# A hybrid encoder layer on one core: block-diagonal matmuls in the DeltaNet recurrence, and where the fifth weight buffer lies

## The chip, the cores and the metric

The kernel runs on one core of one Trainium2 chip. The metric is the device time of one execution in microseconds (us), lower is better; the median of three runs stands for the kernel. The engines are TensorE (PE in the profile, with PEld for its weight loads), VectorE (DVE), ScalarE (ACT), GpSimd (POOL) and SyncE (SP), whose queue issues most of the DMAs.

## The reference

One layer over 16 meta tokens and 512 positions of width 1024, in float32. It is a SwiGLU feed-forward (inner width 2816), a hybrid mixer, and a second feed-forward, each between two RMSNorms and added to the residual `h`:

```
h = h + 0.5 * rmsnorm(swiglu(rmsnorm(h, n[0]), ffn1_wi, ffn1_wo), n[1])
h = h + rmsnorm(hybrid_mixer(rmsnorm(h, n[2]), ...), n[3])
h = h + 0.5 * rmsnorm(swiglu(rmsnorm(h, n[4]), ffn2_wi, ffn2_wo), n[5])
```

The mixer projects its input once, runs a Fourier branch, a short-convolution branch and a gated DeltaNet branch, projects each to 1024, adds them under sigmoid gates and applies one output projection. The DeltaNet branch has 4 heads of 128, runs over chunks of 64 positions, forward and backward in time, and sums the directions. In a chunk, `t` is the inverse of a unit triangular 64x64 matrix, and `attn` is a 64x64 decay-masked attention:

```
def step(S, xs):
    attn_n, u_n, w_n, qd_n, kd_n, gl_n = xs
    v_new = u_n - w_n @ S
    o = qd_n @ S + attn_n @ v_new
    S = S * gl_n[..., None, None] + jnp.swapaxes(kd_n, -1, -2) @ v_new
    return S, o
```

with `u = t @ v_beta` and `w = t @ (k_beta * exp(gc))`.

## The kernel before, in words

**Layout and arithmetic.** Activations lie transposed: channels in 8 blocks of 128 partitions, positions along the free axis. A large matmul is done as three fp32r matmuls: each weight tile and each activation is split into a high part, rounded to fp32r, and a low remainder (`mm`, lines 251 to 257). `load` (line 229) brings a weight tile of 128 x 1024 by DMA into a staging tile `ws` (two buffers), then ACT casts it into `wh` (line 239) and DVE subtracts to get `wl` (line 240). `wh` and `wl` come from the pool `wp`, with five buffers each. All matmuls are issued on line 153, so the profile tells them apart by their tiles: `pb` and `pd` are the two sets of four PSUM banks.

**Order.** PE's instructions run in the order in which the program issues them. The order on the other engines is laid out ahead of time by the tile scheduler from its own cost model, from priorities (`load` is put 150 places ahead, evictions marked urgent further) and from when buffers come free; on the chip each engine then keeps that order and waits at its head. Side work of the mixer (the recurrence, the Fourier transform) is written as generators: `T.at` adds up a modelled PE time for every matmul, and `tick`, called between groups of projection matmuls, resumes a generator once `T.at` has passed the time at which it asked to go on. A `yield SC` asks for 1.8 us after the work issued so far.

**Stages.** The first feed-forward (`ffn`) computes most of its first product by a seven-product (Strassen) scheme over pairs of weight blocks: `pair_load` (line 596) loads two blocks, forms sums on DVE and takes three tile pairs from `wp` and one half-size pair `w4`. `edge` (line 403) crosses to the next stage: it finishes the last output tiles (`tail`), computes the norm, and starts the first products of the next stage with weights (`nxt`) loaded ahead. The mixer follows (`mixer`, line 866), whose units are one weight tile against all positions; then `edge` again, the second feed-forward, and `finish`. Every stage opens pools of its own (`gp` for a feed-forward, `mp` and `dp` for the mixer), which are closed at the edge. In the mixer the eight tiles of the output projection (`A["wout"]`) come last: five in a loop and three in `tail`, in both halves of the positions.

**The recurrence** (`dn_core`, line 1273) runs twice, for heads 0 and 1 and for heads 2 and 3. It builds the masked matrices `A_` and `at` (lines 1323 and 1324), inverts the triangular ones by substitution on DVE into `Z` (which shares the slot `EZ` with earlier tiles, and is named EZ in the profile), and takes eight steps `s`. A step handles four chains: heads `j` = 0, 1 and directions `d` = 0 (chunk `c = s`) and 1 (`c = 7 - s`). Two chunks share the 128 partitions: chunk `c` lies in half `hf = c % 2`, rows `X`, so the two directions of one head are always in opposite halves. A step has three parts with a `yield SC` after each:

- `kq` against the state `Sst` (128x128, four matmuls; the profile's Sst,kq), then `vt` on DVE (line 1450) and the first half of the output `O`;
- four 64x64 matmuls with `Z` (profile: vp,EZ or vn,EZ), then `v1` by four ACT activations that scale by `beta` (line 1465); `vt` and `v1` share the tag `vp`;
- the update of the state, four matmuls of 64 rows by 128 columns with the decayed keys `kd` (tag `sub`; not in the last step), then four 64x64 matmuls with `at`, and the evictions on DVE.

At step 0 the backward chains have no state yet and use `vn` directly.

## Time and profile before

| | |
|---|---|
| median of 3 runs | 1278.52 us (1276.74 to 1278.81) |
| the profiled execution's own time | 1280.05 us |
| its span in the profile | 1278.2 us |
| mean granted TensorE clock | 0.998 |
| DMA | 129.27 MB, mean 101 GB/s |

In the profile a row of a group or of the timeline has the line, the engine, the operation, output<-inputs by tile tags, partitions x elements, and a count. For a matmul the first shape (128\*128, 64\*64, 64\*128) is rows by columns of the array in use. The timeline begins each row with its start and its length in us and ends, where the engine was idle before, with the idle time and what ended it. PE's lengths overlap, since matmuls are pipelined, so costs on PE are read from start to start. An f32 matmul (not fp32r) shows as two records.

### The profile page before, as it was taken

Reading aid. Unit: us, or ns where it says so; the run is one execution under the profiler, and the core shown is the slowest. Engines: PE = TensorE matmul, PEld = TensorE weight load, DVE = VectorE, ACT = ScalarE, POOL = GpSimd, SP = SyncE. Lnnn points to the kernel's source line nnn. Section 1 sums busy time; section 2 is a strip of 40 time slices with the busy share of each in tenths; the row PEclk is TensorE's granted clock in tenths of the full one; section 3 lists DMA queues with packets and bytes.
Section 4 is the critical chain, followed back from the end, with each engine's and each line's share of the span. In section 5 each row is a group of like instructions: output and inputs, shape, how many; then the busy total and the mean of one; then the engine's idle time right before and its main releaser. Section 6 shows DMA issues by size and latency. Waiting matters only on the chain.

```text
span 1278.2 us, 23021 instructions
## 1 busy us (share of the span) xinstructions
PE 1260.2 (99%) x9111; PEld 1155.5 (90%) x9111; DVE 943.3 (74%) x1883; ACT 616.9 (48%) x1201; POOL 13.5 (1%) x28
## 2 busy tenths in 40 slices
PE   9999999999989999999999999999999999999998
PEld 9999999999989988778998777887988999999997
DVE  7978777766568779768799678554779887777654
ACT  7665444434386452344643534334566644444436
POOL 0000000000000000000000000000200000000000
PEclk9999999999999999999999999999999999999999
DMA  7243333321254222422221313235423433333213
GB/s 245 74 143 106 99 99 99 98 96 59 83 187 149 84 78 68 110 77 68 84 67 59 78 48 91 82 94 179 161 87 94 146 100 100 100 100 95 79 50 132
DMA packets 70207, 129.27 MB, mean 101 GB/s; under 512 B 15820, under 2 KB 24140, under 8 KB 70100
## 3 DMA queue, kind: packets, MB, share of 16 engines
q1 hardware_dynamic: 64244, 124.14, 31.1%
q10 hardware_dynamic: 5088, 1.57, 0.5%
q0 software_dynamic: 768, 2.10, 0.4%
q8 instruction: 71, 1.16, 0.4%
q14 instruction: 36, 0.29, 0.1%
HBM read 120.41 MB, written 7.37 MB: 100 GB/s over the span
## 4 chain that ended last, share of the span: by engine, by line
PE 82%; DVE 10%; DMA 2%; ACT 2%; issue 2%; SPq 1%; DVEq 0%; ACTq 0%
PE pb L153 52%; PE pd L153 29%; PE pd L157 1%; DVE wl L245 1%; DMA wf<-in_wi 1%; DVE wl L240 1%; DVE s L414 1%; DVE x L421 1%; DVE acc L312 1%; DVE h L416 1%; DMA ws<-in_wab 1%; ACT wh L239 0%; DVE h L568 0%; DMA h<-in_xT 0%; DMA ws<-in_wout 0%
## 5 line engine op out<-in xcount | busy, mean ns | idle before, releaser
L153 PE MATMUL pb<-x,wh 128*128 128x264 f32 (+3 forms) x1584 | 353.9, 327 | 4.3 <-DVE x L421 1.8
L153 PEld LDWEIGHTS pb<-x,wh 128*128 128x128 f32 x1584 | 247.0, 189 | 33.0 <-issue 4.2
L153 PE MATMUL pb<-x,wl 128*128 128x264 f32 (+3 forms) x792 | 220.4, 323 | 0.0
L153 PE MATMUL pb<-gh,h 128*128 128x264 f32 (+2 forms) x816 | 191.3, 320 | 3.1 <-ACT pb L355 3.1
L153 PE MATMUL pd<-x,wh 128*128 128x264 f32 (+2 forms) x1040 | 192.1, 284 | 0.0
L239 ACT CAST wh<-ws 128x1024 fp32r<-128x1024 f32 (+1 forms) x110 | 105.1, 956 | 170.7 <-PE pb L153 145.7
L244 ACT CAST wh<-wf 128x1024 fp32r<-128x1024 f32 x108 | 113.5, 1051 | 149.2 <-PE pd L153 119.7
L245 DVE TENSOR_TENSOR wl<-wf,wh 128x1024 fp32r<-128x1024 f32 x108 | 131.8, 1222 | 43.4 <-ACT wh L244 42.5
L153 PEld LDWEIGHTS pd<-x,wh 128*128 128x128 f32 x1040 | 160.0, 188 | 1.7
L240 DVE TENSOR_TENSOR wl<-ws,wh 128x1024 fp32r<-128x1024 f32 (+1 forms) x110 | 121.1, 1102 | 37.9 <-ACT wh L239 37.6
L153 PEld LDWEIGHTS pb<-x,wl 128*128 128x128 f32 x792 | 134.6, 188 | 12.4 <-DVE wl L384 0.2
L153 PEld LDWEIGHTS pb<-gh,h 128*128 128x128 f32 x816 | 132.0, 189 | 13.6 <-ACT pb L355 3.7
L153 PE MATMUL pd<-x,wl 128*128 128x264 f32 (+2 forms) x520 | 143.8, 284 | 0.0
L153 PE MATMUL pb<-gl,h 128*128 128x264 f32 (+2 forms) x456 | 123.7, 314 | 0.0
L153 PEld LDWEIGHTS pd<-x,wl 128*128 128x128 f32 x520 | 96.2, 188 | 0.4
L153 PEld LDWEIGHTS pb<-gl,h 128*128 128x128 f32 x456 | 78.3, 189 | 4.3
L153 PE MATMUL pd<-h,wh 128*128 128x264 f32 (+1 forms) x294 | 82.1, 282 | 0.0
L153 PE MATMUL pd<-l,wh 128*128 128x264 f32 (+1 forms) x288 | 81.5, 283 | 0.0
L153 PE MATMUL pd<-h,wl 128*128 128x264 f32 (+1 forms) x288 | 81.4, 283 | 0.0
L698 DVE TENSOR_TENSOR y<-y,pb 128x264 f32<-128x264 f32 (+1 forms) x128 | 48.6, 420 | 30.8 <-PE pb L153 30.8
L239 ACT CAST h<-ws 128x1024 fp32r<-128x1024 f32 (+1 forms) x40 | 38.5, 968 | 60.3 <-PE pb L153 50.5
L153 PE MATMUL pb<-y,wh 128*128 128x512 f32 x192 | 61.3, 400 | 0.0
(325 smaller groups left out, 2295.4 us busy)
## 6 DMA issues: line engine op xcount, KB each, us to landing
wf<-in_wi SPq DMA_DIRECT2D x144, 256.0 KB, 2.6
ws<-in_wo SPq DMA_DIRECT2D x64, 256.0 KB, 3.0
ws<-in_win SPq DMA_DIRECT2D x32, 512.0 KB, 3.6
ws<-in_wg SPq DMA_DIRECT2D x24, 512.0 KB, 3.5
ws<-in_wi SPq DMA_DIRECT2D x13, 512.0 KB, 3.8
ws<-in_wo SPq DMA_DIRECT2D x32, 192.0 KB, 2.4
ws<-in_wout SPq DMA_DIRECT2D x8, 512.0 KB, 3.6
h<-in_xT SPq DMA_DIRECT2D x10, 264.0 KB, 5.3
```

What stands on the lines that cost most here:

```text
L153: return self.e.matmul(out, lhsT, rhs, **kw)
L157: return self.e.transpose(*a)
L239: nc.scalar.copy(h[:, :n], st[:, :n])
L240: nc.vector.tensor_tensor(l[:, :n], st[:, :n], h[:, :n].bitcast(F32), op=ALU.subtract)
L244: self.nc.scalar.copy(h, src)
L245: self.nc.vector.tensor_tensor(l, src, h.bitcast(F32), op=ALU.subtract)
L312: V.tensor_tensor(acc, acc, sq, op=ALU.add)
L414: V.scalar_tensor_tensor(t, ya[0][i][:, k, :W], self.gains[:, gpost, k:k + 1], r[:, c], op0=ALU.mult, op1=ALU.mult)
L416: V.tensor_tensor(hT[:, k, c], hT[:, k, c], t, op=ALU.add)
L421: V.scalar_tensor_tensor(x[1][:, k, c], hT[:, k, c], g, x[0][:, k, c].bitcast(F32), op0=ALU.mult, op1=ALU.subtract)
L698: V.tensor_tensor(y, y, p, op=ALU.add)
```

## The change

It has three parts.

**Blocks on the diagonal.** For one head and step, the forward and the backward 64x64 matrices lie on the diagonal of one 128x128 tile whose other quarters are zero. `at` is laid out so from the start (`[P, 2, 8, P]`, by head and step, cleared on GpSimd, and written in halves). For `Z`, a tile `ZB` (two steps deep) is cleared once, and ACT copies the two blocks of a step into it (`blocks`). `vt` and `v1` then hold both directions of a head in one 128-row tile; where a chain has no state, `vt` is a copy of `vn`. Four 64x64 matmuls become two 128x128 ones, at `Z` and at `at`. `v1` is two activations, scaled by `bB`, which holds `beta` by head and step.

**The weight pool.** `wp` has four buffers in place of five. In a feed-forward, a new function `wtile` takes every fifth tile from the stage's own pool `gp` (tags `wh5` and `wl5`, one buffer) and the others from `wp`; the edge switches this off, and the mixer has the four.

**The tail of the mixer.** The last three output tiles go into three buffers of their own (`th`, `tl`) in the pool `mm` that holds the merged branches.

```
-        self.wp = e(tc.tile_pool(name="wp", bufs=5))
+        self.wp = e(tc.tile_pool(name="wp", bufs=4))
...
+    def wtile(self, tag):
+
+        n = self.turn[tag] = (self.turn.get(tag, 0) + 1) % 5
+        if self.five and n == 0:
+            return self.t(self.gp, tag + "5", [P, KD, P], F32R)
+        return self.t(self.wp, tag, [P, KD, P], F32R)
...
-            h, l = to or (self.t(self.wp, "wh", [P, KD, P], F32R), self.t(self.wp, "wl", [P, KD, P], F32R))
+            h, l = to or (self.wtile("wh"), self.wtile("wl"))
...
+        self.five = False
         tiles, tx, tc, more = tail()
...
+        self.turn, self.five = {}, True
         return ctx
...
-            ws = [(m, self.load(A["wout"][m])) for m in range(KD - NT, KD)]
+            ws = [(m, self.load(A["wout"][m], to=[self.t(self.mm2, i, [P, KD, P], F32R, NT) for i in ("th", "tl")]))
+                  for m in range(KD - NT, KD)]
...
-        at = self.t(dp, "at", B4)
+
+        at = self.t(dp, "at", [P, 2, 8, P])
+        ZB = self.t(dp, "ZB", [P, 2, 2, P])
+        nc.gpsimd.memset(at, 0.0)
+        nc.gpsimd.memset(ZB, 0.0)
...
-                V.tensor_tensor(at[:, 2 * j + d], E[:, 2 * j + d], b[:, :, 1], op=ALU.mult)
+                for hf in range(2):
+                    X = slice(hf * 64, hf * 64 + 64)
+                    V.tensor_tensor(at[X, j, hf::2, X] if d == 0 else at[X, j, 1 - hf::2, X], E[X, 2 * j + d][:, ::1 - 2 * d],
+                                    b[X, ::1 - 2 * d, 1], op=ALU.mult)
...
+        bB = self.t(dp, "bB", [P, 2, 8])
+        for j, d in chains:
+            for hf in range(2):
+                X = slice(hf * 64, hf * 64 + 64)
+                V.tensor_copy(bB[X, j, (hf if d == 0 else 1 - hf)::2], beta[X, 2 * j + d, 0:4][:, ::1 - 2 * d])
+
+        def blocks(s):
+            for d in range(2):
+                c = s if d == 0 else 7 - s
+                X = slice((c % 2) * 64, (c % 2) * 64 + 64)
+                ACT.copy(ZB[X, s % 2, :, X], Z[X, d::2, c // 2])
+        blocks(0)
...
-            vt = self.t(dp, "vp", [P, 4, P], F32, 2)
+            vt = self.t(dp, "vp", [P, 2, P], F32, 2)
...
+                else:
+                    V.tensor_copy(vt[X, j], vn[X, j, t])
...
-            for j, d, hd, c, t, hf, X, Y, has in info:
-                T.matmul(b[X, hd * P:(hd + 1) * P], Z[X, hd, t], vt[X, hd] if has else vn[X, j, t], start=True, stop=True)
-            v1 = self.t(dp, "vp", [P, 4, P], F32, 2)
-            for j, d, hd, c, t, hf, X, Y, has in info:
-                ACT.activation(v1[X, hd], b[X, hd * P:(hd + 1) * P], AF.Copy, scale=beta[X, hd, t:t + 1])
+            for j in range(2):
+                T.matmul(b[:, j * P:(j + 1) * P], ZB[:, s % 2, j], vt[:, j], start=True, stop=True)
+            v1 = self.t(dp, "vp", [P, 2, P], F32, 2)
+            for j in range(2):
+                ACT.activation(v1[:, j], b[:, j * P:(j + 1) * P], AF.Copy, scale=bB[:, j, s:s + 1])
+            if s < 7:
+                blocks(s + 1)
...
-            for j, d, hd, c, t, hf, X, Y, has in info:
-                T.matmul(b[X, hd * P:(hd + 1) * P], at[X, hd, t], v1[X, hd], start=True, stop=True)
+            for j in range(2):
+                T.matmul(b[:, j * P:(j + 1) * P], at[:, j, s], v1[:, j], start=True, stop=True)
```

More of the change, by code (lines that the diff above doesn't have):

```diff
@@ L164, in __init__ @@
         self.sides = []
+        self.turn, self.five = {}, False
         self.T = Tensor(tc.nc)
@@ L371, in start @@
                self.t(self.wp, "wl", [P, KD, P], F32R)) for i in range(len(srcs))]
+        self.turn = {n: len(srcs) for n in ('wh', 'wl')}
         pieces = [slice(0, 1), slice(1, 2), slice(2, 4), slice(4, 6), slice(6, 8)]
@@ L607, in pair_load, with put @@
             nc.sync.dma_start(fc[:, hi], w2[:, hi])
-            def put(f, a, b, w=KD, tag="w", pool=self.wp, bufs=None):
-                h = self.t(pool, tag + "h", [P, w, P], F32R, bufs)
-                l = self.t(pool, tag + "l", [P, w, P], F32R, bufs)
+            def put(f, a, b, w=KD, new=self.wtile):
+                h, l = new(f"w{'4' if w < KD else ''}h"), new(f"w{'4' if w < KD else ''}l")
                 self.split(h, l, f[:, :w])
@@ L622, in pair_load @@
             V.tensor_tensor(fd[:, lo], fb[:, hi], fb[:, lo], op=ALU.add)
-            put(fd, 4, None, 4, "w4", self.gp, 2)
+            put(fd, 4, None, 4, lambda n: self.t(self.gp, n, [P, 4, P], F32R, 2))
         return out
@@ L952, in ready @@
             mm = self.dctx.enter_context(self.tc.tile_pool(name="mm", bufs=1))
+            self.mm2 = mm
             return self.t(mm, "mh", [P, KD, S], F32R), self.t(mm, "ml", [P, KD, S], F32R)
@@ L1449, in dn_core @@
                 if has:
-                    V.scalar_tensor_tensor(vt[X, hd], b[X, hd * P:(hd + 1) * P], neg_eg[X, hd, t:t + 1], vn[X, j, t],
+                    V.scalar_tensor_tensor(vt[X, j], b[X, hd * P:(hd + 1) * P], neg_eg[X, hd, t:t + 1], vn[X, j, t],
                                            op0=ALU.mult, op1=ALU.add)
+                else:
+                    V.tensor_copy(vt[X, j], vn[X, j, t])
             for j, d, hd, c, t, hf, X, Y, has in info:
@@ L1470, in dn_core @@
                 for j, d, hd, c, t, hf, X, Y, has in info:
-                    T.matmul(bS[d][:, j * P:(j + 1) * P], kd[X, (s // 2) % 2, hd], v1[X, hd], start=True, stop=True)
-            for j, d, hd, c, t, hf, X, Y, has in info:
-                T.matmul(b[X, hd * P:(hd + 1) * P], at[X, hd, t], v1[X, hd], start=True, stop=True)
+                    T.matmul(bS[d][:, j * P:(j + 1) * P], kd[X, (s // 2) % 2, hd], v1[X, j], start=True, stop=True)
+            for j in range(2):
+                T.matmul(b[:, j * P:(j + 1) * P], at[:, j, s], v1[:, j], start=True, stop=True)
             if s < 7:
@@ L1481, in dn_core @@
             for j, d, hd, c, t, hf, X, Y, has in info:
-                o = b[X, hd * P:(hd + 1) * P]
+                o = b[X, j * P:(j + 1) * P]
                 if has or not first:
```

## The prediction

> **What bounds the kernel now.** I read the page's busy shares first, then the chain that ended last, then the busy time by stretches of the span.
>
> ```profile
> span 1278.2 us, 23021 instructions
> PE 1260.2 (99%) x9111; PEld 1155.5 (90%) x9111; DVE 943.3 (74%) x1883; ACT 616.9 (48%) x1201; POOL 13.5 (1%) x28
> PE 82%; DVE 10%; DMA 2%; ACT 2%; issue 2%; SPq 1%; DVEq 0%; ACTq 0%
> ```
>
> ```profile
> 60.00:360.00 300.00, 299.67 (x2464) 299.22 (x2463) 214.88 (x310) 139.61 (x239) 0.00 (x0) 1.00 0.32 103
> 540.00:620.00 80.00, 79.93 (x581) 66.63 (x580) 58.94 (x153) 35.64 (x72) 0.00 (x0) 1.00 0.24 73
> 710.00:795.00 85.00, 85.00 (x570) 64.80 (x570) 63.00 (x156) 37.46 (x87) 0.00 (x0) 1.00 0.24 69
> ```
>
> The columns of the second fence are the stretch, its length, then PE, PEld, DVE, ACT and POOL busy, the granted clock, and DMA. The first stretch is most of the first feed-forward; the second and third are where the recurrence's steps run, between the mixer's projection matmuls, once for heads 0 and 1 and once for heads 2 and 3. PE is without a gap in all three, at clock 1.00. So the time is the length of PE's instruction stream plus the few places where PE stands still: PE idles 1278.2 - 1260.2 = 18 us in all. An edit pays if it takes time out of PE's stream, or takes away one of its stalls; work on DVE, ACT and POOL is free until PE waits for it.
>
> **The change: the recurrence's matmuls.** First how many there are. vp names both vt and v1; EZ is the slot that holds Z.
>
> ```profile
> L153 PE MATMUL pd<-vp,at x128: 269/269/320, 548.5 to 791.5; 64*64 64x128 f32 x128
> L153 PE MATMUL pd<-vp,EZ x120: 269/269/320, 545.0 to 788.4; 64*64 64x128 f32 x120
> L1465 ACT ACTIVATE vp<-pd,be x64: 346/363/365, 545.7 to 790.9; 64x128 f32<-64x128 f32 x64
> L153 PE MATMUL pd<-vn,EZ x8: 269/269/320, 545.0 to 721.6; 64*64 64x128 f32 x8
> ```
>
> An f32 matmul leaves two records: 4 matmuls x 8 steps x 2 pairs of heads are 64, and 128 are shown for Z (120 + 8) and for at. The change makes 32 matmuls of 128x128 out of each 64. Durations of pipelined matmuls overlap, so the price must be read from starts. PE's timeline at the first step:
>
> ```profile
> 542.11 0.39 PE L153 MATMUL pb<-y,wl 128*128 128x512 f32 x1
> 542.34 0.61 PE L153 MATMUL pd<-Sst,kq 128*128 128x128 f32 x4
> 542.71 0.71 PE L153 MATMUL pb<-y,wh 128*128 128x512 f32 x2
> 543.25 0.39 PE L153 MATMUL pb<-y,wl 128*128 128x512 f32 x1
> 543.48 0.63 PE L153 MATMUL pb<-x,wh 128*128 128x512 f32 x2
> 543.96 0.39 PE L153 MATMUL pb<-x,wl 128*128 128x512 f32 x1
> ...
> 544.66 0.39 PE L153 MATMUL pb<-x,wl 128*128 128x512 f32 x1
> 544.98 0.32 PE L153 MATMUL pd<-vp,EZ 64*64 64x128 f32 x1
> 544.99 0.32 PE L153 MATMUL pd<-vn,EZ 64*64 64x128 f32 x1
> ...
> 545.57 0.73 PE L153 MATMUL pb<-x,wh 128*128 128x512 f32 x2
> 546.13 0.40 PE L153 MATMUL pb<-x,wl 128*128 128x512 f32 x1
> ...
> 547.54 0.39 PE L153 MATMUL pb<-x,wl 128*128 128x512 f32 x1
> 547.86 0.72 PE L153 MATMUL pd<-vp,sub 64*128 64x128 f32 x8
> 548.51 0.65 PE L153 MATMUL pd<-vp,at 64*64 64x128 f32 x8
> 549.09 0.73 PE L153 MATMUL pb<-x,wh 128*128 128x512 f32 x2
> 549.66 0.39 PE L153 MATMUL pb<-x,wl 128*128 128x512 f32 x1
> ```
>
> A 512-column matmul of the projections starts 0.23 us after the last one (542.11 to 542.34), and two take 0.48 (543.48 to 543.96). Against this pitch a group costs what it adds ahead, its own span, and what the next pair of projection matmuls is late.
>
> Z now: 544.66 to 544.98 is 0.32, so 0.09 ahead; 544.98 to 545.57 is 0.59; 545.57 to 546.13 is 0.56, so 0.08 behind. Sum 0.76 us. The two directions' matmuls do run side by side already (544.98 and 544.99 are its two halves of the array).
>
> Z as two 128x128 matmuls is four records of 128 columns, and this form stands in the same rows: Sst,kq at 542.34, 128*128, x4. It adds nothing ahead, spans 542.34 to 542.71 = 0.37, and the pair behind takes 0.54 (542.71 to 543.25), 0.06 late. Sum 0.43. Saving 0.33 us in each of 16 steps: 5.3 us.
>
> at now follows sub (the update of the state, 64*128, which stays): 548.51 to 549.09 is 0.58, and 0.57 - 0.48 = 0.09 behind: 0.67. As blocks 0.37 + 0.06 = 0.43, if the change of form from sub to at costs the same whether at is 64*64 or 128*128. Saving 0.24 in 14 steps; in the two last steps, without sub, at stands alone like Z and saves 0.33. Together 14 x 0.24 + 2 x 0.33 = 4.0 us.
>
> So 9.3 us leave PE's stream. The bounds: nothing less than the part that hangs on the change of form alone (the second rival, 2.4 us), nothing more than 9.3 plus sub's own change of form, 0.09 in 14 steps, 1.3 us. I take 9.3, since the row of the new form itself is there.
>
> [...]
>
> **The change: what feeds these matmuls.** v1 takes two activations in place of four. Where PE stood still for v1:
>
> ```profile
> 564.89 1.05 ACT L239 CAST wh<-ws 128x1024 fp32r<-128x1024 f32 x1
> ...
> 566.38 1.51 ACT L1465 ACTIVATE vp<-pd,be 64x128 f32<-64x128 f32 x4
> ```
>
> ```profile
> 566.31 0.40 PE L153 MATMUL pb<-y,wl 128*128 128x512 f32 x1
> 566.78 1.65 PE L153 MATMUL pd<-vp,sub 64*128 64x128 f32 x8
> 568.36 0.33 PE L153 MATMUL pd<-vp,at 64*64 64x128 f32 x2
> ```
>
> Here a weight cast stood ahead of v1 on ACT, v1 began at 566.38 and took 1.51 us, and sub took 566.31 to 568.36 = 2.05 up to at, where the undisturbed one takes 547.54 to 548.51 = 0.97: a stall of 1.08. Two activations of 128 partitions have the same free size, so 0.75 in place of 1.51; the stall shrinks to about 0.3. I take 0.7 us; the bounds are 0, if the casts fall otherwise, and 1.1.
>
> New on ACT are two copies a step into ZB, issued behind v1 and ahead of nothing that this step waits for. At the 0.36 of an activation of this shape they are 32 x 0.36 = 12 us, which the 32 activations left out pay for. vt for the missing backward state costs four DVE copies in all, bB sixteen small ones, and at is written in halves:
>
> ```profile
> L1324 DVE TENSOR_TENSOR at<-EZ,pd x8: 401/406/411, 465.8 to 656.3; 128x256 f32<-128x256 f32 x8
> L1350 POOL MEMSET EZ<- x2: 1016/1026/1036, 468.9 to 656.8; 66x1024 f32 x2
> ```
>
> Eight become sixteen with the same elements per partition: 3.2 us more on DVE, before the substitution, whose steps are spaced by PE's own work. Clearing at and ZB, 2048 and 512 elements, is 2.6 us by the memset's row, on POOL, which is busy 1%. I cost these at nothing; without their cover it would be under 2 us at each of the two places. The counter that paces side work falls by 0.43 a group, but each wait is added after the group, so the number of projection matmuls between steps stays.
>
> **The change: weight buffers.** The mixer keeps four pairs in place of five.
>
> ```profile
> L239 ACT CAST wh<-ws x73: 602/1048/1058, 421.7 to 859.0; 128x1024 fp32r<-128x1024 f32 x49, 128x512 fp32r<-128x512 f32 x24
> ...
>   PE pb L153: 132.1, 46
> ```
>
> In the mixer most casts (46 of 73) wait for PE to release a buffer, so the fifth is used; one cast falls on (859.0 - 421.7) / 72 = 6.1 us. A cast, released when the unit four places ahead ends, then has three units, 18 us, until its use, and needs about 1.05 + 1.2. Behind a waiting cast ACT's queue holds v1 and the evictions, but it waits no longer than now, only one unit nearer to the use. I take nothing; the far bound is the rivals' matter. In the feed-forward there are five again, the fifth in the pool of that stage; a pair of units takes three, so a strict turn reaches back nearly two pairs, and PE has no idle time there to win (299.67 of 300): nothing either way.
>
> At the second edge the last three output tiles get buffers of their own, so the next stage's four weights are cast while the output projection runs. Now two of them come in the middle of the edge:
>
> ```profile
> 905.29 1.23 DVE L240 TENSOR_TENSOR wl<-ws,wh 128x1024 fp32r<-128x1024 f32 x1 [1.67 <-ACT wh L239]
> 909.36 1.22 DVE L240 TENSOR_TENSOR wl<-ws,wh 128x1024 fp32r<-128x1024 f32 x1
> ```
>
> ```profile
> 911.02 0.39 PE L153 MATMUL pb<-x,wh 128*128 128x256 f32 x1 [0.47 <-DVE x L421]
> ```
>
> DVE there has no pause, and PE waits for x from it. Taking 2.45 us from DVE's queue can give PE between 0 and 2.45; I take half, 1.2, since the other work closes up. At the first edge PE's longest stall comes from a cast that waits for its data:
>
> ```profile
> 363.57 1.04 ACT L239 CAST wh<-ws 128x1024 fp32r<-128x1024 f32 x1 [1.17 <-DMA ws<-in_wab]
> ```
>
> ```profile
> 366.07 0.39 PE L153 MATMUL pb<-gh,h 128*128 128x264 f32 x1 [2.60 <-ACT pb L355]
> ```
>
> The copy into pb is queued behind that cast. This weight is the fourth, has a buffer in both kernels and waits for its transfer, so I leave the 2.6 us where they are; they may go or grow, since ACT's order is the planner's.
>
> Sum: 9.3 + 0.7 + 1.2 = 11.2 us. The profiled execution took 1280.05, 1.85 over its span and 1.53 over the median of 1278.52; it would become 1268.9, and the median 1267.3.
>
> **Rivals.** (1) The forecast: PE's stream is shorter by about 9 us and the stalls stay or shrink, 1262 to 1271. For it: PE full in both stretches, and the new form priced in the same rows. Chance 0.72. Within it the first edge's 2.6 us may also vanish: 1264.7.
>
> (2) Blocks stream no faster than the pairs. Then Z keeps its 0.59 and loses only 0.09 ahead and 0.02 behind, at 0.03: 16 x 0.11 + 14 x 0.03 + 2 x 0.11 = 2.4 us, and 1276.1. Against it: Sst,kq's 0.37. Chance 0.08, split between faster and same.
>
> (3) The fourth buffer is too few in the mixer: PE finds a weight late by a cast and its subtraction, 2.3 us, at places where short units stand together or ACT is held. Four such places are 9.2 us and take all back: 1277 to 1279. For it: ACT waits 132.1 us for buffers there, so the planner fills every one it has. Against it: 18 us of lead. Chance 0.11.
>
> (4) Slower: a cast stands ahead of v1 in ACT's queue in each step, as at 564.89, because casts come one unit later than now. At 1.08 us in 16 steps this is 17.3 us, less 9.3: 1286.5. It decides from 9.3 / 16 = 0.6 us a step. Against it: v1 is half as long, and the first step (547.54 to 548.51) has no such stall. Chance 0.09.
>
> **How the numbers follow.** About 0.2%, 2.6 us, can be told from no change here. Faster takes rival 1, half of rival 2 (which lies at that bound) and the 0.04 of rival 3 in which less than all is taken back: 0.80. Same is the rest of 2 and 3: 0.11. Slower is rival 4: 0.09. The range runs from 9.3 + 2.45 + 1.1 + 2.6 = 15.5 us of gain, with 1 us for the spread of runs, at 1262, to rival 3's lower end, 1277.
>
> **What would show it.** The changed profile should have 64 records each of vp,ZB and vp,at in form 128*128; Z's four starting 0.23 behind the last projection matmul and spanning about 0.37; at's the same span. Wrong would be a span near 0.59, a stretch from sub to at longer than now (547.86 to 548.51, 0.65), PE waits on wh or wl in the mixer, or v1 behind casts in many steps. The window of the second edge should show the four weights cast before the last output tiles start, and the wait on x shorter.

## The result and the profile after

The changed kernel takes 1272.15 us in the median of five runs (1267.81 to 1273.16); the five runs of the kernel before beside it have 1278.52 (1276.74 to 1279.74). The ratio is 0.9944 [0.9931, 0.9957]: faster by 6.4 us, where 11.2 were forecast. The profiled execution took 1273.16, the longest of the five.

The page of the profile after, its span, busy times and chain:

```profile
span 1271.1 us, 22794 instructions
PE 1252.1 (99%) x8983; PEld 1157.5 (91%) x8983; DVE 952.1 (75%) x1911; ACT 611.6 (48%) x1201; POOL 17.9 (1%) x32
PE 82%; DVE 10%; ACT 3%; DMA 2%; issue 1%; SPq 0%; DVEq 0%; ACTq 0%
```

PE's busy time fell by 8.1 us and PE is still the bound, idle for 19.0 us in place of 18. The two stretches of the recurrence's steps after, with PE, PEld, DVE, ACT, POOL, the granted clock and DMA as before:

```profile
540.00:620.00 80.00, 79.64 (x545) 70.34 (x544) 62.58 (x162) 34.23 (x75) 2.35 (x2) 1.00 0.23 73
710.00:795.00 85.00, 84.68 (x586) 68.84 (x585) 67.11 (x167) 37.66 (x97) 0.00 (x0) 1.00 0.23 72
```

Where before PE lacked 0.07 and nothing in them, it now lacks 0.36 and 0.32. The groups of the new operations, with forms kept apart (busy us, mean ns of one, then idle time of the engine ahead of them):

```profile
L153 PE MATMUL pd<-vp,at 128*128 128x128 f32 x64 | 11.2, 297 | 0.0
L153 PE MATMUL pd<-vp,ZB 128*128 128x128 f32 x64 | 10.9, 285 | 0.5 <-DVE vp L1482 0.5
L1499 ACT ACTIVATE vp<-pd,bB 128x128 f32<-128x128 f32 x32 | 10.0, 362 | 24.3 <-PE pd L153 24.2
L1342 DVE TENSOR_TENSOR at<-EZ,pd 64x256 f32<-64x256 f32 x16 | 6.6, 415 | 0.1
L1459 DVE COPY bB<-be 64x4 f32<-64x4 f32 x16 | 4.3, 266 | 0.2
```

The counts are the forecast ones. (Lines of the changed kernel stand 8 to 34 further down: the cast is L247, its subtraction L248, v1 L1499, vt L1482.) One row stands out at once: a copy of 64x4 elements takes 266 ns in the mean. PE's timeline in the first step after:

```profile
545.49 0.40 PE L153 MATMUL pb<-x,wl 128*128 128x512 f32 x1
545.72 0.61 PE L153 MATMUL pd<-vp,ZB 128*128 128x128 f32 x4
546.08 0.71 PE L153 MATMUL pb<-x,wh 128*128 128x512 f32 x2
546.63 0.39 PE L153 MATMUL pb<-x,wl 128*128 128x512 f32 x1
...
548.34 0.71 PE L153 MATMUL pd<-vp,sub 64*128 64x128 f32 x8
548.99 0.71 PE L153 MATMUL pd<-vp,at 128*128 128x128 f32 x4
549.46 0.71 PE L153 MATMUL pb<-x,wh 128*128 128x512 f32 x2
```

Z starts 0.23 behind the projection matmul (545.49 to 545.72), spans 0.36 (to 546.08), and the pair behind is 0.07 late (0.55 to 546.63): 0.43, as forecast. For `at` the forecast fails: behind sub it spans 548.99 to 549.46 = 0.47, not 0.37.

To see where the 7.1 us of span went, both programs are divided at the starts of the same PE matmuls: (a) to the first projection matmul of the first edge, (b) to the first vmb,km, which opens the first recurrence's steps, (c) to the matmul behind that recurrence's last at, (d) to the second recurrence's first A,const, (e) to its vmb,km, (f) to the matmul behind its last at, (g) to the first 512-column projection of the second feed-forward, (h) to the end. Before, these borders lie at 375.46, 539.52, 616.65, 643.46, 715.76, 791.67 and 938.06. Each cell is the change of the stretch's length in us against the profiled execution before; the kernels below the second row are the experiments.

| kernel | a | b | c | d | e | f | g | h | span |
|---|---|---|---|---|---|---|---|---|---|
| forecast | 0 | 0 | -5.0 | 0 | 0 | -5.0 | -1.2 | 0 | -11.2 |
| after | +1.50 | -0.66 | -3.87 | +1.06 | +3.28 | -4.67 | -3.29 | -0.48 | -7.13 |
| after, run again | -2.69 | -0.68 | -3.86 | +1.05 | +3.20 | -4.65 | -3.59 | -0.50 | -11.71 |
| buffers only | +1.97 | -0.65 | +0.70 | +0.00 | +0.36 | -0.61 | -3.62 | -0.86 | -2.71 |
| Z undone | -0.62 | -0.64 | -1.84 | +0.71 | +3.52 | -2.20 | -3.49 | -0.58 | -5.14 |
| at undone | +0.25 | -0.64 | -2.88 | +0.00 | +0.57 | -3.66 | -3.03 | -0.84 | -10.22 |
| full-width writes | -1.61 | -0.63 | -3.87 | +1.07 | +1.63 | -4.68 | -3.63 | -0.66 | -12.38 |
| cleared once | -0.55 | -0.64 | -3.91 | +0.06 | +2.90 | -4.69 | -3.65 | -0.60 | -11.07 |
| early weight | -1.71 | -0.67 | -3.85 | +1.07 | +3.29 | -4.34 | -3.67 | -0.85 | -10.73 |
| best, no early weight | -0.10 | -0.63 | -3.87 | +0.04 | +0.94 | -4.67 | -3.57 | -0.86 | -12.72 |
| best | -3.28 | -0.66 | -3.91 | +0.06 | +1.04 | -4.68 | -3.63 | -0.84 | -15.90 |
| best, at ahead of sub | -2.88 | -0.63 | -3.92 | +0.06 | +0.95 | -4.99 | -3.32 | -0.85 | -15.58 |
| no tail buffers | -2.72 | -0.64 | -3.89 | +1.06 | +3.27 | -4.69 | +0.38 | -0.40 | -7.64 |
| four in the feed-forward | -0.56 | -0.62 | -3.88 | +1.06 | +3.07 | -4.66 | -3.62 | +2.05 | -7.16 |

Behind column a the cells of unchanged stretches mostly repeat within 0.1 to 0.4 us (e, g and h within 0.7), so single profiles can be compared there; column a cannot (see the first edge, below). The intervals of most single-edit kernels' ratios overlap the changed kernel's, so what one edit is worth is read from the stretches and not from the medians. Behind it the change won 8.63 us: 8.5 in the steps (c and f), 4.4 at the edges and in the second feed-forward (b, g, h), less 4.3 lost between the two recurrences (d and e).

### The profile page after: what moved, and what is told of

Read it like the earlier page. It is cut to its first block, busy times and chain, and to the rows that moved or that the text cites. A ratio compares the mean times of both kernels' runs of the same rounds, so it can differ in the third digit from the quotient of the medians.

```text
span 1271.1 us, 22794 instructions
## 1 busy us (share of the span) xinstructions
PE 1252.1 (99%) x8983; PEld 1157.5 (91%) x8983; DVE 952.1 (75%) x1911; ACT 611.6 (48%) x1201; POOL 17.9 (1%) x32
## 4 chain that ended last, share of the span: by engine, by line
PE 82%; DVE 10%; ACT 3%; DMA 2%; issue 1%; SPq 0%; DVEq 0%; ACTq 0%
PE pb L153 50%; PE pd L153 32%; DVE wl L248 2%; PE pd L157 1%; DMA ws<-in_win 1%; DMA ws<-in_wab 1%; DVE vp L1482 1%; DVE x L430 1%; ACT wh L247 1%; DVE s L423 1%; DVE t L551 0%; DVE h L425 0%; ACT sy L348 0%; DMA h<-in_xT 0%; DVE O L1520 0%
## 5 line engine op out<-in xcount | busy, mean ns | idle before, releaser
L247 ACT CAST wh<-ws 128x1024 fp32r<-128x1024 f32 (+1 forms) x107 | 101.7, 952 | 138.7 <-PE pb L153 108.7
L248 DVE TENSOR_TENSOR wl<-ws,wh 128x1024 fp32r<-128x1024 f32 (+1 forms) x107 | 117.5, 1099 | 25.8 <-ACT wh L247 25.6
L247 ACT CAST h<-ws 128x1024 fp32r<-128x1024 f32 (+1 forms) x40 | 38.5, 968 | 59.4 <-PE pb L153 50.5
```

Of the source, the lines that this page charges most:

```text
L247: nc.scalar.copy(h[:, :n], st[:, :n])
L248: nc.vector.tensor_tensor(l[:, :n], st[:, :n], h[:, :n].bitcast(F32), op=ALU.subtract)
```

## Experiments: the steps themselves

The theory after the first reading was that the steps and the edge had won about what was forecast, and that the preparation of the second recurrence, costed at nothing, had taken 4.3 back. The rival was that the weight pool, with four buffers, had taken it.

**The buffers alone.** The kernel before with only the change's buffer parts:

```
-        self.wp = e(tc.tile_pool(name="wp", bufs=5))
+        self.wp = e(tc.tile_pool(name="wp", bufs=4))
...
+            ws = [(m, self.load(A["wout"][m], to=[self.t(self.mm2, i, [P, KD, P], F32R, NT) for i in ("th", "tl")]))
```

> The kernel before with only the two buffer parts of the change (four pairs in the pool, the fifth in the feed-forward's pool, the tail's own three); the recurrence is the old one. My theory: the gain at the second edge and at the mixer's end (3.4 us in the traces) and the 1.5 us of the feed-forwards come from the buffers, the 4.3 us lost between the two recurrences do not, and the first edge still loses up to 2.2: 1274 to 1276, with 99.1 us from the last at of the first recurrence to the second one's vmb,km, as before. Rival: the four buffers cost the 4.3 us in the mixer: that stretch takes 103 us and the time is 1278 to 1280.

It took 1275.67 (1273.66 to 1277.63, 12 runs), ratio 0.9978 [0.9968, 0.9987]. Its d and e are +0.36 in sum: the 4.3 are not the buffers'. They do move casts about in the steps: +0.70 in c, -0.61 in f. One such place is common to this kernel and the changed one; DVE and PE after, at the second Z:

```profile
552.69 1.23 DVE L248 TENSOR_TENSOR wl<-ws,wh 128x1024 fp32r<-128x1024 f32 x1 [0.16 <-ACT wh L247]
```

```profile
554.72 0.49 PE L153 MATMUL pd<-vp,ZB 128*128 128x128 f32 x2
555.47 0.49 PE L153 MATMUL pd<-vp,ZB 128*128 128x128 f32 x2 [0.26 <-DVE vp L1482]
555.71 0.71 PE L153 MATMUL pb<-y,wh 128*128 128x512 f32 x2
```

A full weight's subtraction stands ahead of vt on DVE, vt ends late, and Z takes 554.72 to 555.71 = 0.99 in place of 0.36. This is rival 4 in small, on DVE instead of ACT and in one step of eight.

**The inverses undone.** Only Z's matmuls go back to four of 64x64; all else as changed.

```
-                T.matmul(b[:, j * P:(j + 1) * P], ZB[:, s % 2, j], vt[:, j], start=True, stop=True)
+                T.matmul(b[X, j * P:(j + 1) * P], Z[X, hd, t], vt[X, j], start=True, stop=True)
```

> The changed kernel with one thing undone: the product with the inverses is four 64x64 matmuls again, written into the new layout (ZB is still filled, and not read). By the starts in the traces each group costs 0.33 us more: 16 x 0.33 = 5.3, so 1277.5, with Z's eight records spanning 0.58. If the change of form were free, or the gain lay in v1 and vt alone, the time would stay at 1272.

1274.55 (1272.74 to 1276.73, 8 runs), ratio 0.997 [0.9958, 0.9981]; c and f grow by 2.03 and 2.47, so Z's blocks are worth 4.5 us. PE's timeline of this kernel:

```profile
543.73 0.65 PE L153 MATMUL pd<-vp,EZ 64*64 64x128 f32 x8
544.31 0.73 PE L153 MATMUL pb<-x,wh 128*128 128x512 f32 x2
```

The pairs of 64\*64 span 0.58 again (543.73 to 544.31): rival 2 (blocks stream no faster) is out.

**The attention undone.** `at` is 64x64 per head and chunk again, four full-width writes, no clearing, four matmuls of 64*64.

```
-                for hf in range(2):
-                    X = slice(hf * 64, hf * 64 + 64)
-                    V.tensor_tensor(at[X, j, hf::2, X] if d == 0 else at[X, j, 1 - hf::2, X], ...)
+                V.tensor_tensor(at[:, 2 * j + d], E[:, 2 * j + d], b[:, :, 1], op=ALU.mult)
...
-                T.matmul(b[:, j * P:(j + 1) * P], at[:, j, s], v1[:, j], start=True, stop=True)
+                T.matmul(b[X, j * P:(j + 1) * P], at[X, hd, t], v1[X, j], start=True, stop=True)
```

> The changed kernel with the attention part undone: at is again one 64x64 tile per head, direction and chunk, written by four full-width DVE operations, without its clearing, and multiplied by four 64*64 matmuls a step; the inverses stay blocks. Theory: at's blocks save 0.14 us behind sub in 14 steps and 0.33 in two, 2.6 us in all, or 1.3 a recurrence, and cost 1.65 us where the halved writes hold the PSUM banks and about 1.0 where the clearing of at holds a bB copy: so each recurrence grows by 1.3, the stretch up to the second A,const shrinks by 1.0 and the one up to vmb by 1.6, and the sum is the same time within 1 us, 1271 to 1273. Rival: the forecast's own term, 4.0 us saved and nothing paid for it: 1276. A second rival: the loss between the recurrences is the inverses' part too (the vt copies, bB and ZB); then those two stretches stay as they are and the kernel is 2.6 us slower, 1274.7.

1268.0 (1266.32 to 1271.88, 6 runs), ratio 0.9921 [0.9901, 0.994], not slower than the changed kernel but, in the medians, 4.1 faster (the intervals overlap). c and f grow by 0.99 and 1.01, so `at`'s blocks win 2.0 in the steps, half of the forecast 4.0 (in `at`'s own rows, read from start to start, it is 2.6, the theory's size, and 0.5 goes back at Z's matmuls, which wait longer for vt); and d and e shrink from 4.34 to 0.57, so they cost 3.8 in the preparation. As changed, the attention half of the change is a loss of 1.8 us; the theory had 2.6 for 2.6. What the medians show beyond 1.8 is not in the stretches behind the first edge. The timeline of this kernel, the first `at`:

```profile
547.76 0.66 PE L153 MATMUL pd<-vp,at 64*64 64x128 f32 x8
548.35 0.72 PE L153 MATMUL pb<-x,wh 128*128 128x512 f32 x2
```

Behind sub, `at` as 64\*64 spans 0.59 and as 128\*128 0.47, while Z, with no sub ahead, spans 0.58 as 64\*64 and 0.36 as 128\*128. So the change of form from 64\*128 to 128\*128 costs 0.1 more than the one from 64\*128 to 64\*64.

**`at` ahead of sub.** If that change of form is the price, it might be avoided by issuing `at` first. On top of the best version (below):

```
+            for j in range(2):
+                T.matmul(b[:, j * P:(j + 1) * P], at[:, j, s], v1[:, j], start=True, stop=True)
             if s < 7:
                 bS = [self.dnp(), self.dnp()]
...
-            for j in range(2):
-                T.matmul(b[:, j * P:(j + 1) * P], at[:, j, s], v1[:, j], start=True, stop=True)
```

> The best version with one thing more: in each step at's two matmuls are issued ahead of the state's update (sub) instead of behind it, so that at stands directly behind a projection matmul of its own form and sub between at and the next projection matmul. Theory: what at's blocks saved less than forecast behind sub (0.14 a step, not 0.24) is the change of form from 64*128 to 128*128, which costs 0.1 more than the one from 64*128 to 64*64. Ahead of sub, at's four records start 0.23 behind the projection matmul and span 0.37; then sub pays its 0.09 ahead, its 0.65, and the 0.1 to 0.2 of the change back: at and sub together take about 1.2 us over the pitch, against 1.29 now, so 0.05 to 0.15 in 14 steps: 0.7 to 2 us faster than the best version's 1264.6. Rival: a change of form costs the same wherever it lies, since there are two of them either way: no difference. Second rival: the state's update comes 0.4 us later in each step and the next step's product with it waits: slower by up to 0.4 in 14 steps, 1270.

1264.31 (1264.03 to 1266.47, 4 runs), ratio 0.9899 [0.9883, 0.9916], against 1264.59 and 0.9896 of the best version: no difference, the first rival. Its timeline:

```profile
543.93 0.61 PE L153 MATMUL pd<-vp,at 128*128 128x128 f32 x4
544.47 0.71 PE L153 MATMUL pd<-vp,sub 64*128 64x128 f32 x8
```

`at` takes 0.54 up to sub (543.93 to 544.47), where the form alone takes 0.36: the price has moved to the border on the other side of `at`.

## Experiments: what the blocks cost between the recurrences

**Full-width writes.** The half writes of `at`, on DVE, ahead of the second recurrence; the same place before, and then after:

```profile
654.30 0.40 DVE L1324 TENSOR_TENSOR at<-EZ,pd 128x256 f32<-128x256 f32 x1
654.63 0.40 DVE L1323 TENSOR_TENSOR A<-A,pd 128x256 f32<-128x256 f32 x1
```

```profile
653.77 0.84 DVE L1342 TENSOR_TENSOR at<-EZ,pd 64x256 f32<-64x256 f32 x2
654.62 0.42 DVE L1339 TENSOR_TENSOR A<-A,pd 128x256 f32<-128x256 f32 x1
```

A write of A and its write of `at` took 0.66 together (two rows of 0.33 from start to start) and now take 1.2, four times over. PE at that place has only the Fourier transform's short matmuls, and they wait. PE before, and then after:

```profile
654.84 2.09 PE L153 MATMUL pd<-tabz,zfold 128*128 128x134 f32 x16
...
658.03 0.73 PE L153 MATMUL pb<-x,wh 128*128 128x264 f32 x4
```

```profile
652.87 1.18 PE L153 MATMUL pd<-tabz,zfold 128*128 128x134 f32 x8
654.52 1.18 PE L153 MATMUL pd<-tabz,zfold 128*128 128x134 f32 x8 [0.47 <-ACT t L1059]
...
657.41 0.94 PE L153 MATMUL pd<-const,t 128*128 128x128 f32 x6 [0.62 <-ACT zfold L1050]
658.10 0.73 PE L153 MATMUL pb<-x,wh 128*128 128x264 f32 x4
```

From the first row to the last this took 3.19 and now takes 5.23, 2.0 of the 3.28 in e. Whether PE feels DVE's longer queue or the PSUM banks of kq, which stay taken longer, is not told apart. The edit computes `at` in place in `E` by four full-width operations and lets POOL copy the halves into the blocks:

```
+                V.tensor_tensor(E[:, 2 * j + d], E[:, 2 * j + d], b[:, :, 1], op=ALU.mult)
                 for hf in range(2):
                     X = slice(hf * 64, hf * 64 + 64)
-                    V.tensor_tensor(at[X, j, hf::2, X] ..., E[X, 2 * j + d][:, ::1 - 2 * d], b[X, ::1 - 2 * d, 1], op=ALU.mult)
+                    nc.gpsimd.tensor_copy(at[X, j, hf::2, X] ..., E[X, 2 * j + d][:, ::1 - 2 * d])
```

> The changed kernel, but at is computed in place by four full-width DVE instructions per pair of heads, as before, and GpSimd copies the halves into the blocks. My theory: the halved writes hold the PSUM banks of the kq products 1.7 us longer on DVE, and PE's Fourier matmuls behind them wait; with four writes the waits at 653 to 657 go, and the time falls by 1.5 to 2.5 us below the changed kernel, to about 1270. Rival: the waits there come from the order on ACT, and the stretch and the time stay at 1272.

1269.1 (1266.57 to 1270.41, 6 runs), ratio 0.9925 [0.9912, 0.9939]; e falls from 3.28 to 1.63, so the half writes cost 1.65 there. The wait that is left at this place, 0.9, ends with a DVE write that reads kq's product out of PSUM, which speaks for the banks but does not show it. POOL needs 3.5 us for the copies, and none of PE's seven longest waits (0.9 us and more) is put down to them.

**Cleared once.** DVE and POOL at the end of the first recurrence after; the second recurrence's copies into bB have been laid out ahead to here, and so has its clearing of `at`:

```profile
613.71 2.95 DVE L1459 COPY bB<-be 64x4 f32<-64x4 f32 x7
```

```profile
613.92 1.81 POOL L1303 MEMSET at<- 128x2048 f32 x1 [2.01 <-PE pd L153]
```

The rows of the tile bB give 98/167/1872 ns as least, median and most: of the seven copies one takes 1.87 us and ends where the clearing ends. Behind the copies DVE holds the convolution (L1071, L1072), behind that ACT has a silu and the squares of the keys (L1269), and PE waits for these at a transpose of the keys:

```profile
633.49 0.65 PE L157 MATMUL pd<-ident,kn 128*128 128x128 f32 x4 [0.93 <-ACT sq L1269]
```

To tell the clearing from the copies, `at` and ZB are allocated and cleared only ahead of the first recurrence; the quarters off the diagonal stay zero.

```
-        nc.gpsimd.memset(at, 0.0)
-        nc.gpsimd.memset(ZB, 0.0)
+        if r == 0:
+            ...
+            nc.gpsimd.memset(self.at, 0.0)
+            nc.gpsimd.memset(self.ZB, 0.0)
+        at, ZB = self.at, self.ZB
```

> The changed kernel with at and ZB allocated and cleared once, ahead of the first recurrence, and used again in the second (the quarters off the diagonal are never written, so they stay zero). Theory: in the changed kernel the second clearing (1.81 us on POOL from 613.92) lies on top of one of the sixteen small copies into bB, which takes 1.87 us in place of 0.16, and the convolution's chain on DVE behind it is late by that, which PE feels as the 0.9 us stall of the transpose of km at 632.3. Then the seven copies take about 1.2 us in place of 2.95, that stall goes, the stretch from the end of the first recurrence to the second one's first matmul (A,const) is 0.9 to 1.1 us shorter than in the changed kernel, and everything else stands: about 1271. Rival A: the copies themselves or where the planner puts them are the cause; then the stretch keeps its 27.9 us. Rival B: the clearing also delays the second recurrence's own preparation; then the stretch up to the second vmb, 3.3 us longer than before the change, shrinks too, by 1 us or more.

1268.22 (1266.5 to 1269.42, 6 runs), ratio 0.992 [0.9904, 0.9935]. DVE's timeline of this kernel:

```profile
611.66 1.24 DVE L1461 COPY bB<-be 64x4 f32<-64x4 f32 x7
```

The copies are where they were and take 1.24; d falls from 1.06 to 0.06, and the wait on sq is gone from PE's waits. So in d it was the clearing, not the copies. Rival B, which had 1 us or more in e, is not shown by this run: e is 0.38 lower, and kernels with the same preparation spread from 3.07 to 3.52 there. On top of the full-width writes, clearing once takes 0.6 to 0.7 off e (1.63 to 0.94 and 1.04, the two best kernels, below). The median fell by more than these 1.4 us; of the rest, 2.05 lie in column a of the two profiles.

## Experiments: edges and feed-forward

**No tail buffers.** The last three output tiles go through the four common pairs.

```
-            ws = [(m, self.load(A["wout"][m], to=[self.t(self.mm2, i, [P, KD, P], F32R, NT) for i in ("th", "tl")]))
+            ws = [(m, self.load(A["wout"][m]))
```

> The changed kernel without the buffers of their own for the last three output tiles: these weights go through the four common pairs again. Theory: all that the second edge and the output projection won (0.8 to 1.2 us ahead of the last tiles, 2.57 between the last tile and the first unit of the second feed-forward) comes from these buffers: 3.4 to 3.8 us slower, about 1275.8, and by the forecast's half of DVE's 2.45 us only 1.2 slower, 1273.4. Rival: with one buffer pair fewer than before and none of its own, two casts in the edge become three, and it is slower by more than the change won, 5 us or more: 1277. Other rival: the gain came from the strict turn in the feed-forward's pools; then no difference.

1273.64 (1272.86 to 1276.04, 11 runs), ratio 0.9966 [0.9955, 0.9977]. In the trace g is +0.38 in place of -3.59 of the run again: the buffers are worth 4.0 us, of which before had some, since it had a fifth pair (the rival's point, with its size smaller). In the medians it is only 1.5 to 1.6; column a is low in this profile, and most of its runs lie above it, but that does not bring the two figures together. DVE's subtractions of weights in the edge show why. Before there were three (905.29, 909.36 and one more at 917.28), without the tail buffers there are four (896.57, 900.63, 902.90, 909.46); after there is one:

```profile
910.30 1.22 DVE L248 TENSOR_TENSOR wl<-ws,wh 128x1024 fp32r<-128x1024 f32 x1
```

```profile
880.99 1.05 ACT L247 CAST wh<-ws 128x1024 fp32r<-128x1024 f32 x1 [1.36 <-DMA ws<-in_wi]
...
889.43 1.05 ACT L247 CAST wh<-ws 128x1024 fp32r<-128x1024 f32 x1 [0.54 <-DMA ws<-in_wi]
```

The second fence, ACT's, has the first and the last of the next stage's four casts. The last output tiles start at 888.05, so three casts lie ahead of them, as forecast, and the fourth 1.4 us behind their start, well ahead of the edge's first projection at 906.18. PE's waits on x from DVE, 0.47 and 0.38 at the same place before, are no longer there.

**Four in the feed-forward.** The fifth buffer of that stage is not used.

```
-        self.turn, self.five = {}, True
+        self.turn, self.five = {}, False
```

> The changed kernel with four weight buffers in the feed-forwards, in place of the fifth taken from that stage's own pool in a strict turn; all else as changed. Theory, the forecast's: PE has no idle time in the feed-forward to win and a strict turn reaches back nearly two pairs either way, so the fifth is worth nothing there: same time as the changed kernel within 0.5 us outside the two edges. Rival A: a pair of units takes three weights, so with four the next pair's third cast waits for PE's release of the pair under way, and PE stands still once a pair: 1 us in each of some 30 pairs, slower than before the change, 1300 or more. Rival B: only the edges, where five casts come together, feel it: 1 to 3 us slower there.

1274.09 (1272.98 to 1275.54, 5 runs), ratio 0.9965 [0.9952, 0.9978], 2.1 above the changed kernel run beside it. h is +2.05 in place of -0.50: the fifth buffer is worth 2.6 us in the second feed-forward. PE's stalls there, which the changed kernel does not have:

```profile
966.54 0.39 PE L153 MATMUL pd<-h,wl 128*128 128x256 f32 x1 [0.76 <-DVE wl L253]
974.20 0.39 PE L153 MATMUL pd<-x,wh 128*128 128x256 f32 x1 [0.45 <-DVE x L253]
```

They are 1.2 of the 2.6. They come in the first units after the edge, not in every pair: neither the forecast's nothing nor rival A's 30 us, but the size of rival B.

**The first edge, and the changed kernel once more.**

> The changed kernel itself once more, beside the two runs below on one chip. Theory: stage by stage its profile repeats the first one within 0.1 us behind the first edge, and only the two stages up to the first edge move, by lots of half clock of 3.4 us, each of which costs some 1.7 us; so the median lies between 1269 and 1273. Rival: the time of 1272.15 is the kernel's own and the versions that came out near 1268 differ from it by more than their edits show; then it repeats 1272 within 0.6 us.

1272.0 (1268.69 to 1273.07, 5 runs), ratio 0.9947 [0.9932, 0.9961]: the median repeats, as the rival had it, and the stretches behind the first edge repeat within 0.3, where the theory had 0.1; but its profiled execution took 1268.69, 4.5 less than the first. Of that, 4.2 is column a. PE at the end of the first feed-forward, in the first profile, and then in the second:

```profile
366.08 0.59 PE L153 MATMUL pb<-gh,h 128*128 128x264 f32 x1 [3.21 <-ACT pb L363]
```

```profile
364.94 0.39 PE L153 MATMUL pb<-gh,h 128*128 128x264 f32 x1 [1.69 <-ACT pb L363]
```

The copy into pb is queued behind the cast of the gates' weight, which waits for its transfer; that wait was 1.82 in the one and 0.27 in the other. And the granted clock of the 7 us that follow, first and second:

```profile
366.00:373.00 7.00, 6.92 (x34) 6.92 (x35) 1.76 (x5) 3.57 (x13) 0.00 (x0) 0.52 0.22 76
```

```profile
366.00:373.00 7.00, 7.00 (x59) 7.00 (x59) 5.02 (x15) 6.60 (x21) 0.00 (x1) 1.00 0.19 67
```

That the mean of 0.52 is half clock for nearly all of the stretch shows in a stretch inside it:

```profile
367.00:370.00 3.00, 3.00 (x17) 3.00 (x16) 0.52 (x3) 1.43 (x5) 0.00 (x0) 0.50 0.49 167
```

In the first PE ran at half clock for 7 x 0.48 x 2 = 6.7 us, with 34 matmul records in the 7 us in place of 59, and lost by estimate half of that, 3.4. The stall is 1.5 longer; together 4.9, of which column a shows 4.2. To take the stall away, the weight is loaded ahead through a staging buffer of its own:

```
+            with self.tc.high_priority(AHEAD):
+                st = self.t(self.gp, "wf", [P, KD, P], F32, 5)
+            self.wab = self.load(self.A["wab"], st=st)
...
-        o = self.unit(A["wab"], x, ALLC)
+        o = self.unit(self.wab, x, ALLC)
```

> The changed kernel, but the mixer's first weight (wab) is staged in an idle buffer of the feed-forward's pool, so that its transfer is issued ahead of the residual's eight. My theory: its cast no longer waits at the head of ACT's queue, PE's stall of 3.2 us goes, and with it the 6 us of half-speed matmuls behind: 5 to 6.5 us less, 1266, clock 0.999 in every run and a spread of runs under 2 us. Rival: the slow matmuls have another cause; then only the stall goes, 3 us, and the spread stays.

1268.86 (1267.89 to 1270.95, 6 runs), ratio 0.9928 [0.9915, 0.994]: 3.3 under the changed kernel, where the theory had 5 to 6.5 and a spread under 2 (it is 3.1). The long stall is gone, but the two shorter ones left, 0.85 and 0.97, were followed by half clock in this profile:

```profile
358.96 0.59 PE L153 MATMUL pb<-gh,h 128*128 128x264 f32 x1 [0.97 <-ACT pb L364]
```

```profile
358.80:362.40 3.60, 3.44 (x16) 3.44 (x17) 1.32 (x4) 2.95 (x10) 0.00 (x0) 0.53 0.93 370
```

**The best version** has three edits together: cleared once, full-width writes, early weight.

> The changed kernel with three edits together: at and ZB cleared once; at computed in place by four full-width DVE operations for each pair of heads, with POOL copying the halves into the blocks; the gates' weight loaded at the first edge through a staging buffer of its own. Theory: 1.65 us for the writes and 1.0 for the clearing come off, and the first edge's 2.6 us stall with them; since the two runs with one of these edits came out at 1268.9 and 1269.1 partly through the first edge's half clock, which comes and goes in lots of 3.4 us, the sum is 1266 to 1268. Rival: POOL's copies collide with DVE as the clearing did and give the gain back: 1269 or more.

1264.59 (1263.82 to 1266.2, 5 runs), ratio 0.9896 [0.9879, 0.9912]: 13.7 us faster than before and 7.6 than the change. d and e are 1.10 in sum in place of 4.34, so the rival's collision does not show. Without the early weight:

> The best version so far (1264.59) without its early load of the gates' weight: at and ZB cleared once, at in place by full-width operations with POOL copying the halves. Theory: the early load takes away the first edge's 2.6 us stall and one lot of half clock in most runs, so without it 2.6 to 4.3 us slower, 1267 to 1269; against the changed kernel the two edits left bring 1.0 + 1.65 to 2.0, seen in the stretches between the recurrences as in the best version. Rival: the half clock comes as often without the stall's weight load, and the early load is worth at most its 1.2 us of waiting: 1266.

1266.33 (1265.07 to 1267.59, 4 runs), ratio 0.9903 [0.9887, 0.9918]. So the early weight is worth 1.7 in the medians here and 3.3 on the changed kernel, with intervals that overlap; the rival's 1266 is the nearer.

## Why the prediction was right or wrong

- **What bounds the kernel**: right. PE is the bound in both, and every cell of the table is read from PE's starts.
- **Z's blocks**, 5.3 us: right in mechanism and in the price of an undisturbed step (0.76 to 0.43); 4.5 by undoing them. The prediction looked for no wait on vt: Z spans 0.99 in place of 0.36 at two of the sixteen steps after and 0.48 to 0.54 at three more, 1.7 us in all, where before it was late at one step, by 0.8.
- **`at`'s blocks**, 4.0 us: the clause "if the change of form from sub to at costs the same whether at is 64\*64 or 128\*128" failed. It costs 0.1 more, 2.0 are left of 4.0. The bounds for `Z` and `at` together, 2.4 to 10.6, had the 6.5 inside them.
- **v1**, 0.7 us: right in mechanism (an activation of 128x128 took 362 ns in the median after, one of 64x128 363 before), too small in size. At the quoted place sub now takes this long, from the row ahead of it to `at`,

```profile
566.55 0.40 PE L153 MATMUL pb<-y,wl 128*128 128x512 f32 x1
...
567.73 0.71 PE L153 MATMUL pd<-vp,at 128*128 128x128 f32 x4
```

  1.18 in place of 2.05, 0.87 won. But sub stood waiting for v1 at other steps too. Its spans from start to start, summed over the 14 steps, were 10.49 before and are 9.06 after, and 9.06 and 9.03 in the two undone kernels, which keep the two activations: 1.4 us, twice the term and above its bound of 1.1. Before, the last `at` waits for v1 as well (0.81 in place of 0.58). Together they are most of what Z undone and at undone leave of c and f, 8.54 - 4.50 - 2.00 = 2.0.
- **"I cost these at nothing"**: this is the step that failed. The prediction gave "under 2 us at each of the two places" without cover. Ahead of the first recurrence the cover held (b is the same with and without the blocks: -0.66 and -0.65). Between the recurrences it did not, at 4.3 us: 1.65 from the half writes, 1.0 in d and some 0.4 to 0.7 in e from the clearing, 0.36 in the buffers-only kernel. With both edits d and e still lose 0.98 to 1.10, so beyond the 0.36 about 0.7 is not isolated. The words "whose steps are spaced by PE's own work" were true of the substitution and not of what stands ahead of it, where PE is given short matmuls that wait for DVE. And DVE's row of the copies beside a clearing stood in the trace before:

```profile
656.84 1.02 POOL L1350 MEMSET EZ<- 66x1024 f32 x1 [136.88 <-DVE Am L1328]
```

```profile
656.75 0.21 DVE L1338 COPY Ad<-A 32x128 f32<-32x128 f32 x1
...
657.12 0.81 DVE L1338 COPY Ad<-A 32x128 f32<-32x128 f32 x1
```

  One copy of 0.2 us took 0.81 while POOL cleared. A busy share of 1% on POOL did not tell that its work would hold DVE.
- **The second edge**, half of DVE's 2.45 us: the mechanism was right and the size too small. Stretch g won 3.3 to 3.6; the stretch from the edge's first projection matmul to the second feed-forward alone won 2.57 (27.79 to 25.22), all of DVE's 2.45 and a little more. Another 0.8 to 1.2 came ahead of the last output tiles; it is there in the buffers-only kernel and without the tail buffers alike. Of it, 0.64 are two waits of PE at the start of the output projection, on mh (0.41) and ml (0.23), which only the kernel before has; why they went is open.
- **The mixer's four buffers at nothing**: right in sum (+0.70 and -0.61); rival 3's waits on wh or wl did not come. **The fifth buffer in its turn at nothing**: wrong by a small size, h won 0.5 to 0.9 against the plain five and would have lost 2.05 with four.
- **The first edge left as it is**: it stayed where it was, but it is not constant. Behind it 8.6 to 9.0 us are won in the two profiles, of which the medians show 5.9 to 6.4. The mean granted clock was 0.9968 over the ten runs of the changed kernel and 0.9979 over 44 runs of before. If all of the difference fell on PE's work, it would be 0.0011 x 1272 = 1.4 us; that is an estimate from above, since the mean also holds half clock behind PE's last matmul, where it costs nothing (the last 4.0 us of the span after, 2.9 before, which alone is 0.0004). That the changed kernel meets the half clock more often fits, but where it falls in runs without a profile can't be seen, and why is open.

Together, against the forecast 11.2: steps -1.5, preparation -4.3, edges and feed-forwards +3.2, which makes 8.6 behind the first edge; and 2.2 that the median lacks of it. So the time fell into the range partly by luck: a loss that the prediction did not count was in part made up by gains that it did not count either, and the upper part of the range, where the median lies, had been left for rival 3, which did not come.

## What to carry to other kernels

When an edit shortens matmuls on the bounding engine, price its preparation stage by stage: the same kind of half writes was free ahead of one recurrence (b, -0.66 with the blocks and -0.65 without) and cost 1.65 us ahead of the other, where PE has nothing long to do. A clearing on an idle engine was not free here where it lay beside small copies of another (1.87 us for a copy of 0.17); clear once and keep the zeros. And price a group of matmuls with what stands ahead of it: the same four records took 0.36 behind their own form and 0.47 behind another.

## What the runs showed of the hardware

A POOL memset of 128x2048 elements held a DVE copy of 64x4 elements for its whole 1.81 us (1.87 in place of 0.167), and beside one of 66x1024, 1.02 us long, a copy took 0.81 in place of 0.21. The same clearing, ahead of the first recurrence at 377.3, ran beside DVE operations with two tensor inputs whose length did not change (0.43 and 0.49). Why the copies were held and these operations were not, no row shows.

The half clock came in lots: 6.7 us after, and before the window from 367.30 shows one of 3.60 x 0.47 x 2 = 3.4, the same as in the early-weight kernel:

```profile
367.30:370.90 3.60, 3.60 (x20) 3.60 (x19) 1.53 (x3) 2.31 (x7) 0.00 (x0) 0.53 0.34 127
```

What sets their length and what brings them on was not shown. Stalls of 2.60 before and of 0.97 in the early-weight kernel (with one of 0.85 ahead of it) were followed by one, and one of 1.69, in the changed kernel run again, was not. The length of the stall alone does not decide it: one of 1.87, in the best version without the early weight, was followed by half clock (mean 0.96 from 360 to 400 us), and one of 2.50, without the tail buffers, was not (1.00).
